# Queries, keys and values by one level of Strassen's recursion in a one-core streaming step

## The chip, the core and the metric

The kernel runs on one of the eight cores of a Trainium2 chip. The metric is the device time of one execution, in microseconds (us). A core has a matrix engine (TensorE, PE in the rows; PEld is its weight load), three engines for elementwise work (VectorE, DVE; ScalarE, ACT; GpSimd, POOL), and SyncE (SP), which here only issues DMAs. Matmul results land in PSUM; everything else lies in the on-chip SBUF or in DRAM.

## The reference

One layer of a hybrid encoder, for 2048 prompt tokens and 64 sample tokens (2112 in all), width 1024. The normalised input is multiplied by one wide weight, and the products feed two branches:

```python
xn = rms_norm(x, norm_gain)
u = xn @ w_in
xa, za, q, k, v, zb, ga, gb = split_in(u)          # 1024 columns each
...
q = rms_norm(q.reshape(B, T, H_B, 2, DK), q_norm_gain)   # groups of 64 columns
k = rms_norm(k.reshape(B, T, H_B, 2, DK), k_norm_gain)
v = v.reshape(B, T, H_B, DV)
...
m = jax.nn.sigmoid(ga) * (ya @ w_proj_a) + jax.nn.sigmoid(gb) * (yb @ w_proj_b)
y = x + m @ w_out
```

`ya` is a gated linear recurrence over `xa`, `yb` an eight-head differential attention over `q`, `k`, `v`. Everything is float32; k and v are outputs too.

## The kernel before

Each float32 operand is split into a rounded high part and a remainder, x = hi + lo, and each product is three matmuls (hi·hi, hi·lo, lo·hi): `mm3`, L68 to L71. The program has four stages: (A) L142 to L349, queries, keys and values; (B) L351 to L496, the five other column blocks and the recurrence; then the attention and the output projections. The change touches A and the first lines of B.

**Stage A.** 17 tiles of 128 tokens (the last has 64). Each is loaded (`norm_x`, L161), normalised, transposed by TensorE in eight pieces into PSUM (`turn_x`, L179) and split by ACT and DVE into `xh`, `xl`, which stay in SBUF through stage B. The weight comes in 12 blocks of 256 columns (`load_w`, L150): blocks 0 to 2 and 3 are values, 4 to 11 hold queries and keys of one head each. The order is 0, 1, 2, 4 to 11, 3 (L317). Per block and tile there are 8 slices of the contraction times 3 passes, 256 columns each: 12 × 17 × 24 = 4896 matmuls into the PSUM tile `acca`, which holds two token tiles. Values are copied out (L341, L342). Queries and keys are normalised per 64 columns (`norm_qk`, L200: square on ACT, sum on DVE, square root on ACT, reciprocal, a Newton step and a product on DVE), then transposed by TensorE (`turn_qk`, L226) and split into what the attention reads. The list `prev` holds one normalised accumulator back: the transposes of an accumulator are issued after the matmuls of the next one (L345).

**Stage B.** For each of eight groups n of 128 columns, five weights of 128 columns (`load_w1`, L357) meet the five token groups of `GROUPS` (512, 512, 384, 384, 320 wide) in `accb`: `hawk` for xa and za, and `gated` for zb, ga, gb (L489 to L494).

**Order.** TensorE's instructions run in the order in which the code emits them (`manual_schedule`, L113). The scheduler orders the other engines; SP takes the loads and stores in one queue, and an entry whose wait is not met holds back those behind it.

## Time and profile before

| | us |
|---|---|
| median of 3 runs | 3071.75 (3069.01 to 3071.79) |
| span of the profiled execution, first to last instruction | 3068.5 |
| stage A, first to last start of a matmul into `acca` | 14.0 to 662.3 |
| stage B, first to last start into `accb` | 663.2 to 1630.7 |
| TensorE busy | 2982.8 (97%) |
| DVE, ACT, POOL busy | 1322.6, 1135.1, 1065.5 |

The profiled execution's time is its span and some 3 us around it; the median of the runs stands 3.25 us above the span. A matmul's busy time overlaps its neighbours', so the distance between two starts, the pitch, is what one costs.

### The profile page before, as it was taken

How to read it: one execution, taken by the hardware profiler on the slowest of the kernel's cores; microseconds unless marked ns; L12 is line 12 of the kernel's file. 1: busy time of each engine (PE TensorE's matmuls, PEld its weight loads, DVE VectorE, ACT ScalarE, POOL GpSimd, SP SyncE). 2: the span in 40 equal slices, each digit the busy share in tenths (PEclk: the TensorE clock that was granted, in tenths of full speed). 3: DMA queues.
4: the chain of work that ended last, by engine and by line, in shares of the span. 5: the costliest groups of instructions: out<-in, count | busy, mean ns of one | idle time of the engine just before them, and what ended most of it. 6: DMA issues, size and time to landing. Idle time of an engine off the chain costs nothing.

```text
span 3068.5 us, 50185 instructions
## 1 busy us (share of the span) xinstructions
PE 2982.8 (97%) x19448; PEld 2787.9 (91%) x19448; DVE 1322.6 (43%) x3439; ACT 1135.1 (37%) x2179; POOL 1065.5 (35%) x1011
## 2 busy tenths in 40 slices
PE   7999999999999999999998999999999989999999
PEld 7999999999999998999896888888888889999999
DVE  7015454413314224133135667767776761232311
ACT  5112222213224223223134766676676651110100
POOL 1113233222212222122114666666666652222220
PEclk9999999999999999999999999999999999999999
DMA  5223333322121121121117344444543343433322
GB/s 173 81 83 115 125 124 129 120 83 72 39 75 58 43 83 50 45 77 42 64 47 212 107 143 128 127 138 135 147 115 123 94 155 110 122 118 90 94 94 91
DMA packets 208350, 312.37 MB, mean 102 GB/s; under 512 B 33760, under 2 KB 132944, under 8 KB 208112
## 3 DMA queue, kind: packets, MB, share of 16 engines
q1 hardware_dynamic: 203264, 299.10, 30.6%
q0 software_dynamic: 2608, 8.91, 1.0%
q8 instruction: 154, 2.52, 0.3%
q10 hardware_dynamic: 2240, 1.15, 0.1%
q14 instruction: 84, 0.69, 0.1%
HBM read 203.53 MB, written 105.41 MB: 101 GB/s over the span
## 4 chain that ended last, share of the span: by engine, by line
PE 84%; DVE 7%; ACT 3%; issue 2%; DMA 2%; POOL 1%; SPq 0%; POOLq 0%; ACTq 0%; DVEq 0%
PE accb L71 8%; PE accb L70 8%; PE accb L69 8%; PE acca L69 6%; PE acca L70 6%; PE acca L71 6%; PE acc L71 6%; PE acc L69 6%; PE acc L70 6%; PE accv L640 6%; PE pk L574 3%; PE pk L575 3%; PE ptt L632 3%; PE accv L763 2%; PE pk L695 1%
## 5 line engine op out<-in xcount | busy, mean ns | idle before, releaser
L71 PE MATMUL accb<-xh,wl 128*128 128x512 f32 (+2 forms) x1600 | 562.5, 352 | 0.0
L69 PE MATMUL accb<-xh,wh 128*128 128x512 f32 (+2 forms) x1600 | 562.3, 351 | 0.0
L70 PE MATMUL accb<-xl,wh 128*128 128x512 f32 (+2 forms) x1600 | 562.2, 351 | 0.0
L69 PE MATMUL acca<-wh,xh 128*128 128x256 f32 (+1 forms) x1632 | 469.1, 287 | 0.0
L70 PE MATMUL acca<-wl,xh 128*128 128x256 f32 (+1 forms) x1632 | 461.7, 283 | 2.1 <-DVE wl L131 1.6
L71 PE MATMUL acca<-wh,xl 128*128 128x256 f32 (+1 forms) x1632 | 461.3, 283 | 0.0
L71 PE MATMUL acc<-gh,wl 128*128 128x352 f32 x1152 | 373.6, 324 | 0.0
L69 PE MATMUL acc<-gh,wh 128*128 128x352 f32 x1152 | 373.1, 324 | 0.0
L70 PE MATMUL acc<-gl,wh 128*128 128x352 f32 x1152 | 370.8, 322 | 0.0
L69 PEld LDWEIGHTS accb<-xh,wh 128*128 128x128 f32 x1600 | 300.4, 188 | 25.6
L70 PEld LDWEIGHTS accb<-xl,wh 128*128 128x128 f32 x1600 | 300.3, 188 | 25.5
L71 PEld LDWEIGHTS accb<-xh,wl 128*128 128x128 f32 x1600 | 300.3, 188 | 25.3
L69 PEld LDWEIGHTS acca<-wh,xh 128*128 128x128 f32 (+1 forms) x1632 | 307.7, 189 | 5.4 <-ACT vst L341 3.8
L70 PEld LDWEIGHTS acca<-wl,xh 128*128 128x128 f32 (+1 forms) x1632 | 307.8, 189 | 2.8 <-DVE wl L131 1.8
L71 PEld LDWEIGHTS acca<-wh,xl 128*128 128x128 f32 (+1 forms) x1632 | 307.5, 188 | 0.0
L640 PE MATMUL accv<-v,tw 128*128 128x128 f32 x2176 | 295.3, 278 | 6.3 <-ACT o L652 6.2
L574 PE MATMUL pk<-k,Q 128*128 128x512 f32 (+2 forms) x640 | 266.3, 417 | 29.6 <-DVE mp L595 19.9
L56 POOL TENSOR_SCALAR wh<-raw 128x512 fp32r<-128x512 f32 x125 | 81.7, 654 | 607.9 <-PE accb L70 364.6
L587 DVE TENSOR_SCALAR_CACHE_REDUCE S<-pk,far 128x1024 f32<-128x1024 f32 x224 | 225.8, 1014 | 141.4 <-PE pk L575 131.5
L640 PEld LDWEIGHTS accv<-v,tw 128*128 128x128 f32 x2176 | 270.7, 194 | 10.9 <-ACT o L652 8.3
L605 ACT ACTIVATE S<-S,nm 128x1920 f32<-128x1920 f32 (+7 forms) x128 | 209.0, 1633 | 74.8 <-DVE nm L604 73.3
L575 PE MATMUL pk<-k,Q 128*128 128x512 f32 (+2 forms) x640 | 232.8, 369 | 1.0 <-DMA Q<-ql_d 1.0
(230 smaller groups left out, 5059.3 us busy)
## 6 DMA issues: line engine op xcount, KB each, us to landing
raw<-in_w1b SPq DMA_DIRECT2D x80, 256.0 KB, 2.9
raw<-in_ckT SPq DMA_DIRECT2D x32, 512.0 KB, 4.2
raw<-in_cv SPq DMA_DIRECT2D x32, 512.0 KB, 4.1
Q<-qh_d SPq DMA_DIRECT2D x126, 128.0 KB, 2.8
Q<-ql_d SPq DMA_DIRECT2D x126, 128.0 KB, 2.8
raw<-in_w1a SPq DMA_DIRECT2D x46, 256.0 KB, 3.0
gt<-ga_d SPq DMA_DIRECT2D x48, 176.0 KB, 2.6
rg<-yb_d SPq DMA_DIRECT2D x24, 352.0 KB, 3.1
```

What stands on the lines that cost most here:

```text
L56: nc.gpsimd.tensor_scalar(hi, src, 1.0, 1.0, op0=ALU.mult, op1=ALU.mult)
L69: nc.tensor.matmul(out, shi, mhi, start=start, stop=False)
L70: nc.tensor.matmul(out, shi, mlo, start=False, stop=False)
L71: nc.tensor.matmul(out, slo, mhi, start=False, stop=stop)
L574: nc.tensor.matmul(pk[:, o], Q[0][:, m, qs], kk, start=True, stop=False)
L575: nc.tensor.matmul(pk[:, o], Q[1][:, m, qs], kk, start=False, stop=True)
L587: nc.vector.tensor_scalar(s[:, k0 : k0 + f], pk[:, :f], far[:, h : h + 1], None, op0=ALU.add, op1=ALU.max, accum_out=mp[:, cx["j"] : cx["j ...
L605: nc.scalar.activation(s[:, :n], s[:, :n], AF.Exp, bias=nm, accum_out=sc[m])
L632: nc.tensor.transpose(ptt[:, j, :], ss[r][:, kt * P : (kt + 1) * P], ident)
L640: nc.tensor.matmul(acc[:, r, :], tw[:, j, :], hd[kt // 8][1][:, kt % 8, :], start=kt == r == 0, stop=kt == 2 * p + 1)
L695: nc.tensor.matmul(pk[:, us], Q, kc[:, us], start=True, stop=True)
L763: nc.tensor.matmul(acc, tw[:, j, :], vc[:, (j8 % 2) * 4 + j, :], start=j8 == 0 and j == 0, stop=False)
```

## The change

Values, and then queries with keys of heads 0 to 3 and of heads 4 to 7, become three groups g of 1024 columns. In each group the weight (1024 × 1024) and a pair of token tiles (t and t + 8) are cut into quarters: A11, A12 (tile t, first and second half of the contraction), A21, A22 (tile t + 8), B11 to B22. Seven products of sums and differences of quarters replace eight. A product is 4 slices × 3 passes = 12 matmuls of 512 columns. Eight pairs × 7 × 12 × 3 groups = 2016 matmuls; the sample's tile goes by the plain product, 60 matmuls in each group, 2196 in all. The order inside a group is `ITEMS` = 0, 1, 2, 3, "s", 4, 5, 6, 7.

The sums of quarters (S1 to S4 of x, T1 to T4 of the weight) are made on DVE and POOL and split again. `pair` issues the seven products; after each comes `fill`, which emits pieces of work that is due: steps of the next item's x (`x_steps`), at the end of a group steps of the next group's weight (`weight_steps`), and one entry of the list `later`, which holds the transposes of queries and keys. `done` is called as each of the four results C22, C11, C21, C12 comes up; for queries and keys one norm covers all four. In group 0 the normalised, transposed x is written to DRAM as `xn_d`; groups 1 and 2 read it back (`fetch_x`), and so does stage B (`take_x`), which now computes zb, ga and gb of n = 0 first, token group by token group. TensorE has 136 transposes of x, 272 of queries and keys and 8 small products (`strip_out`) in stage A, before and after.

```diff
+    xn_d = dram.tile([NT, P, KT, P], F32, name="xn_d")
...
+            wq = c.enter_context(tc.tile_pool(name="wq", bufs=17))
+            xo = c.enter_context(tc.tile_pool(name="xo", bufs=20))
+            sb = c.enter_context(tc.tile_pool(name="sb", bufs=13))
...
+            pm = c.enter_context(tc.tile_pool(name="pma", bufs=5, space=PSUM))
+            pt = c.enter_context(tc.tile_pool(name="pta", bufs=3, space=PSUM))
...
+            def cut(raw, fast, parts=2):
+                n = 4 // parts
+                hi = wq.tile([P, 4, 512], F32R, name="w8")
+                lo = wq.tile([P, 4, 512], F32R, name="w8")
+                for i in range(parts):
+                    s = slice(i * n, i * n + n)
+                    nc.scalar.copy(hi[:, s, :], raw[:, s, :])
+                    eng = nc.vector if fast or i % 2 == 0 else nc.gpsimd
+                    eng.tensor_tensor(lo[:, s, :], raw[:, s, :], hi.bitcast(F32)[:, s, :], op=ALU.subtract)
+                return hi, lo
...
+            def weight_steps(g, ws, fast):
+                src = I["wg"][g]
+                q = {}
+                parts = 4 if fast else 2
+                n = 4 // parts
+                def load(nm, i):
+                    q[nm] = quarter()
+                    for k in range(0, 4, 2):
+                        nc.sync.dma_start(q[nm][:, k : k + 2, :], src[i, :, k : k + 2, :])
...
+                return [
+                    lambda: load("B11", 0),
+                    lambda: load("B12", 1),
+                    lambda: sub("T1", "B12", "B11"),
+                    lambda: halve("B11", "B11"),
+                    lambda: load("B22", 3),
+                    lambda: load("B21", 2),
+                    lambda: sub("T2", "B22", "T1"),
+                    lambda: sub("T4", "B21", "T2"),
+                    lambda: halve("T2", "T2"),
+                    third,
+                    lambda: halve("T3", "T3"),
+                    lambda: halve("T1", "T1"),
+                    lambda: halve("B21", "B21"),
+                    lambda: halve("T4", "T4"),
+                    lambda: halve("B22", "B22"),
+                ]
...
+            def turn_x(t, half):
+                xt = xs[t][half]
+                ptx = pt.tile([P, 4, P], F32, name="ptx")
+                for j in range(4):
+                    nc.tensor.transpose(ptx[:, j, :tn], xt[:tn, j * P : (j + 1) * P], ident[:tn, :tn])
+                o = xo.tile([P, 4, P], F32, name="xq")
+                nc.vector.tensor_tensor(
+                    o[:, :, :tn], ptx[:, :, :tn],
+                    gain[:, half * 4 : half * 4 + 4].unsqueeze(2).to_broadcast([P, 4, tn]), op=ALU.mult,
+                nc.sync.dma_start(xn_d[t, :, half * 4 : half * 4 + 4, :tn], o[:, :, :tn])
+                return o
+            def fetch_x(t, half):
+                o = xo.tile([P, 4, P], F32, name="xq")
+                nc.sync.dma_start(o[:, :, :tn], xn_d[t, :, half * 4 : half * 4 + 4, :tn])
+                return o
...
+            def x_steps(item, first, xo_):
...
+                return [
+                    lambda: put("A11", lo, 0),
+                    lambda: put("A21", hi, 0),
+                    lambda: put("A22", hi, 1),
+                    lambda: (add(V, "S1", "A21", "A22", ALU.add), put("A12", lo, 1)),
+                    lambda: (add(V, "S2", "S1", "A11", ALU.subtract), s3()),
+                    lambda: (sp("A11", G), add(G, "S4", "A12", "S2", ALU.subtract)),
+                    lambda: (sp("S2", V), sp("S3", G)),
+                    lambda: (sp("S1", G), sp("A12", V), sp("A22", G), sp("S4", G)),
+                ]
+            def product(out, a, b, start, stop, m=P, more=False):
+                for kt in range(4):
+                    mm3(nc, out, a[0][:, kt, :m], a[1][:, kt, :m], b[0][:, kt, :], b[1][:, kt, :],
+                        start and kt == 0, stop and kt == 3, more)
...
+            def pair(x, w, done, fill):
+                b1 = pm.tile([P, 512], F32, name="acc")
+                product(b1, x["A11"], w["B11"], True, True)
+                p1 = small()
+                nc.scalar.copy(p1, b1)
+                fill()
+                b2 = pm.tile([P, 512], F32, name="acc")
+                product(b2, x["S2"], w["T2"], True, True)
+                u2 = small()
+                nc.vector.tensor_tensor(u2, p1, b2, op=ALU.add)
+                fill()
+                b3 = pm.tile([P, 512], F32, name="acc")
+                product(b3, x["S3"], w["T3"], True, True)
+                u3 = small()
+                nc.vector.tensor_tensor(u3, u2, b3, op=ALU.add)
+                fill()
+                b4 = pm.tile([P, 512], F32, name="acc")
+                product(b4, x["S1"], w["T1"], True, True)
+                c22 = small()
+                nc.vector.tensor_tensor(c22, u3, b4, op=ALU.add)
+                done(1, 1, c22)
+                fill()
+                product(b1, x["A12"], w["B21"], False, True, more=True)
+                c11 = small()
+                nc.scalar.copy(c11, b1)
+                done(0, 0, c11)
+                fill()
+                product(b3, x["A22"], w["T4"], False, True, more=True)
+                c21 = small()
+                nc.vector.tensor_tensor(c21, u2, b3, op=ALU.add)
+                done(1, 0, c21)
+                fill()
+                product(b4, x["S4"], w["B22"], False, True, more=True)
+                c12 = small()
+                nc.vector.tensor_tensor(c12, u2, b4, op=ALU.add)
+                done(0, 1, c12)
+                fill()
...
+            def out_qk(g, item):
+                h0 = 4 * (g - 1)
+                nb = 2 if item == "s" else 4
+                got = []
+                v = wk.tile([P, 32], F32, name="va")
+                def done(r, half, c):
+                    t = NT - 1 if item == "s" else item + 8 * r
+                    tn = TOK[t][1]
+                    sqv = small()
+                    nc.scalar.activation(sqv[:tn], c[:tn], AF.Square)
+                    i = len(got)
+                    nc.vector.tensor_reduce(
+                        v[:tn, 8 * i : 8 * i + 8], sqv[:tn].rearrange("p (g d) -> p g d", d=DK), axis=AX.X, op=ALU.add
+                    )
+                    got.append((half, t, c))
+                    if len(got) < nb:
+                        return
...
+                    for i, (isk, t, c) in enumerate(got):
+                        cv = c[:tn].rearrange("p (g d) -> p g d", d=DK)
+                        nc.vector.tensor_tensor(
+                            cv, cv, y[:tn, 8 * i : 8 * i + 8].unsqueeze(2).to_broadcast([tn, 8, DK]), op=ALU.mult
+                        )
+                        later.append(lambda isk=isk, t=t, c=c: turn_qk(h0, isk, t, c))
+                return done
...
+            norm_x(0)
+            norm_x(8)
+            wst = weight_steps(0, W[0], True)
+            for fn in wst[:2]:
+                fn()
+            X[0, 0] = {}
+            xst = x_steps(0, True, X[0, 0])
+            for fn in xst:
+                fn()
+            for fn in wst[2:]:
+                fn()
+            for g in range(NG):
+                for i, it in enumerate(ITEMS):
+                    nxt = (g, i + 1) if i + 1 < len(ITEMS) else (g + 1, 0)
+                    todo = []
+                    if nxt[0] < NG:
+                        X[nxt] = {}
+                        nit = ITEMS[nxt[1]]
+                        if nxt[0] == 0:
+                            for t in tiles_of(nit):
+                                norm_x(t)
+                        todo = x_steps(nit, nxt[0] == 0, X[nxt])
+                    if g + 1 < NG and i == 7:
+                        wnext = weight_steps(g + 1, W[g + 1], False)
+                        for fn in wnext[:3]:
+                            fn()
+                    more = wnext[3:] if g + 1 < NG and i == 8 else []
...
+                    def fill():
+                        for _ in range(2):
+                            if more:
+                                more.pop(0)()
+                        for _ in range(2 if nxt[0] > 0 else 1):
+                            if todo:
+                                todo.pop(0)()
+                        run_later()
+                    out = (out_v if g == 0 else out_qk)(g, it)
+                    (sample if it == "s" else pair)(X.pop((g, i)), W[g], out, fill)
+                    while more or todo:
+                        fill()
...
+            def take_x(g):
+                g0, gw = GROUPS[g]
+                for t in range(g0 // P, (g0 + gw + P - 1) // P):
+                    t0, tn = TOK[t]
+                    raw = hk.tile([P, 1092], F32, name=("R", "IX", "A")[t % 3])[:, : KT * P]
+                    raw = raw.rearrange("p (k t) -> p k t", k=KT)[:, :, :tn]
+                    nc.sync.dma_start(raw, xn_d[t, :, :, :tn])
+                    o = slice(t0 - g0, t0 - g0 + tn)
+                    nc.scalar.copy(xh[g][:, :, o], raw)
+                    nc.vector.tensor_tensor(xl[g][:, :, o], raw, xh[g].bitcast(F32)[:, :, o], op=ALU.subtract)
...
+            GATED = ((2, zb_d, True), (3, ga_d, False), (4, gb_d, False))
+            take_x(0)
+            w0 = [load_w1(j) for j, _, _ in GATED]
+            for g in range(1, len(GROUPS)):
+                take_x(g)
+            for g in range(len(GROUPS)):
+                for w, (j, dst, silu) in zip(w0, GATED):
+                    gate_out(mm_grp(w, g), dst, 0, silu, g)
+                hawk(n, load_w1(5 * n), load_w1(5 * n + 1))
...
+    wg = [quar(col(v, 0, 4), col(v, 4, 4))] + [quar(col(q, h, 4), col(k, h, 4)) for h in (0, 4)]
```

The end of a pair of queries and keys, on TensorE, before (an accumulator's end; `acca_2995` is two token tiles, `vst_2980` is the normalised accumulator before it):

```order
L70 MATMUL acca_2995<-wl_2820,xh1_99 128x256
L71 MATMUL acca_2995<-wh_2819,xl1_100 128x256
L232 MATMUL ptx_3059<-ident_70,vst_2980 128x128 [waits DVE_49,PE_49,Activation_49]
L232 MATMUL ptx_3059<-ident_70,vst_2980 128x128 x3
L69 MATMUL acca_3074<-wh_2801,xh1_99 128x256 [waits Activation_49]
L70 MATMUL acca_3074<-wl_2802,xh1_99 128x256
L71 MATMUL acca_3074<-wh_2801,xl1_100 128x256
```

And now: `acc_2491` takes the pair's last product, `s2_2504` is the same pair's C22, normalised, and `acc_2617` the next pair's first product.

```order
L70 MATMUL acc_2491<-w8_2144,xq_2308 128x512
L71 MATMUL acc_2491<-w8_2145,xq_2308 128x512
L72 MATMUL acc_2491<-w8_2144,xq_2309 128x512
L359 MATMUL ptx_2602<-ident_71,s2_2504 128x128 [waits DVE_49,PE_49]
L359 MATMUL ptx_2602<-ident_71,s2_2504 128x128 x3
L70 MATMUL acc_2617<-w8_1975,xq_2471 128x512
L71 MATMUL acc_2617<-w8_1976,xq_2471 128x512
L72 MATMUL acc_2617<-w8_1975,xq_2472 128x512 [waits Pool_49]
```

Before, the four transposes stood behind the matmuls of the next accumulator; now they stand right behind the last product of their own pair, and the next pair's products behind them.

The work of DVE at that place: from C12 (`s2_2584`), read from the last product, over the sums, the root and the Newton step to the normalised C22 (`s2_2504`).

```order
L322 TENSOR_TENSOR s2_2584<-s2_2434,acc_2491 128x512 [waits DMAHW3_49,PE_49]
L253 TENSOR_TENSOR xq_2694<-xq_2664,xq_2632 128x512 [waits DMAHW0_49,DVE_49]
L389 TENSOR_REDUCE va_2390<-s2_2586 128x8 [waits Activation_49]
L396 TENSOR_SCALAR va_2390<-va_2390 128x32 [waits DVE_49]
L401 RECIPROCAL ya_2592<-sra_2590 128x32 [waits Activation_49]
L62 SCALAR_TENSOR_TENSOR tmpa_2593<-ya_2592 128x32 [waits DVE_49]
L63 TENSOR_TENSOR tmpa_2593<-tmpa_2593,va_2390 128x32 [waits DVE_49]
L64 SCALAR_TENSOR_TENSOR ya_2592<-tmpa_2593,ya_2592 128x32 [waits DVE_49]
L405 TENSOR_TENSOR s2_2504<-s2_2504,ya_2592 128x512 [waits DVE_49]
```

C22's product with its norm now stands behind the last of the four results.

SP in the middle of the values, before: loads of x (`big`) two at a time ahead of the stores of values.

```order
L342 DMA out_v<-vst_453 128x512 [waits DMAHW1_49,Activation_49]
L164 DMA big_623<-in_x 128x1024 [waits DVE_49,PE_49]
L164 DMA big_681<-in_x 128x1024 [waits DMAHW3_49,DVE_49,PE_49]
L342 DMA out_v<-vst_565 128x512 [waits DMAHW4_49,Activation_49]
L164 DMA big_735<-in_x 128x1024 [waits DMAHW5_49,DVE_49,PE_49]
L164 DMA big_793<-in_x 128x1024 [waits DMAHW6_49,DVE_49,PE_49]
```

Now: `s2_500` and `s2_521` are C21 and C12 of one pair; `s2_548`, `s2_549` are the two halves of a tile of the second pair after it, and `s2_569`, `s2_570` those of its partner eight tiles on.

```order
L349 DMA out_v<-s2_500 128x2x256 [waits DMAHW4_49,DVE_49]
L197 DMA s2_548<-in_x 128x512 [waits DMAHW5_49]
L349 DMA out_v<-s2_521 128x2x256 [waits DMAHW6_49,DVE_49]
L197 DMA s2_549<-in_x 128x512 [waits DMAHW7_49,PE_49]
L197 DMA s2_569<-in_x 128x512 [waits DMAHW0_49,PE_49]
L197 DMA s2_570<-in_x 128x512 [waits DMAHW1_49,PE_49]
L223 DMA xn_d_67<-xq_610 128x512 [waits DMAHW2_49,DVE_49]
```

Three of the four halves stand behind the store of C12. On TensorE the transposes of `s2_548` follow the first product of the pair that comes next (`acc_590`); both halves go into the norm that they wait for.

SP at the passage to stage B: the last stores of keys and queries, the first weights of stage B (`raw`), and the reads of `xn_d` into `R`, `IX` and `A`.

```order
L375 DMA ql_d_58<-s2_6026 128x4x128 [waits DMAHW3_49,DVE_49]
L375 DMA out_kT<-s2_6036 128x4x128 [waits DMAHW4_49,Activation_49]
L375 DMA kh_d_59<-s2_6037 128x4x128 [waits DMAHW5_49,Pool_49]
L375 DMA kl_d_60<-s2_6038 128x4x128 [waits DMAHW6_49,Pool_49]
L532 DMA raw_6123<-in_w1b 128x512 [waits DMAHW7_49]
L532 DMA raw_6129<-in_w1b 128x512 [waits DMAHW0_49]
L673 DMA R_6083<-xn_d_67 128x1024 [waits DMAHW1_49]
L673 DMA IX_6087<-xn_d_67 128x1024 [waits DMAHW2_49]
L673 DMA A_6091<-xn_d_67 128x1024 [waits DMAHW3_49,PE_49]
L532 DMA raw_6612<-in_w1b 128x512 [waits DMAHW7_49,DMAHW4_49,Pool_49]
L532 DMA raw_6618<-in_w1b 128x512 [waits DMAHW5_49,DMAHW0_49,Pool_49]
L673 DMA R_6095<-xn_d_67 128x1024 [waits DMAHW6_49,DMAHW1_49,DVE_49]
```

Before, no x was read there; now the first three tiles stand behind the stores, and the fourth also behind the release of `R` by DVE.

## Rows read from the trace of the kernel before

**Rows 1.** The page, parts 1 and 4: busy time of each engine; the chain by engine.
```profile
PE 2982.8 (97%) x19448; PEld 2787.9 (91%) x19448; DVE 1322.6 (43%) x3439; ACT 1135.1 (37%) x2179; POOL 1065.5 (35%) x1011
...
PE 84%; DVE 7%; ACT 3%; issue 2%; DMA 2%; POOL 1%; SPq 0%; POOLq 0%; ACTq 0%; DVEq 0%
```

**Rows 2.** Tile acca: duration in ns min/median/max, first and last start, forms.
```profile
L69 PE MATMUL acca<-wh,xh x1632: 276/283/562, 14.0 to 662.1; 128*128 128x256 f32 x171, 128*64 128x256 f32 x11
```

**Rows 3.** The same view of tile accb.
```profile
L69 PE MATMUL accb<-xh,wh x1600: 305/334/499, 663.2 to 1630.4; 128*128 128x512 f32 x71, 128*128 128x384 f32 x71, 128*128 128x320 f32 x36
```

**Rows 4.** Timeline of PE at 300 us: start, duration, engine, line, instruction.
```profile
299.90 0.28 PE L69 MATMUL acca<-wh,xh 128*128 128x256 f32 x1
...
302.78 0.28 PE L69 MATMUL acca<-wh,xh 128*128 128x256 f32 x1
```

**Rows 5.** Timeline of PE at the start of the second stage.
```profile
664.01 0.40 PE L69 MATMUL accb<-xh,wh 128*128 128x512 f32 x1
...
667.42 0.39 PE L69 MATMUL accb<-xh,wh 128*128 128x512 f32 x1
```

**Rows 6.** Chain of waits, 0 to 60 us: start, duration, what.
```profile
2.60 7.96 DMA gain<-in_gain
...
32.89 1.07 PE ptx L186 x8
...
40.59 0.87 PE ptx L186 x8
```

**Rows 7.** Timeline of ACT at 533 us.
```profile
533.21 0.60 ACT L205 ACTIVATE sqa<-acca 128x512 f32<-128x512 f32 x1 [3.87 <-PE acca L71]
...
535.38 0.20 ACT L212 ACTIVATE sra<-va 128x8 f32<-128x8 f32 x1
```

**Rows 8.** Timeline of DVE at 533 us.
```profile
533.85 0.69 DVE L207 TENSOR_REDUCE va<-sqa 128x8 f32<-128x512 f32 x1 [2.51 <-ACT sqa L205]
...
536.05 0.17 DVE L63 TENSOR_TENSOR tmpa<-tmpa,va 128x8 f32<-128x8 f32 x1
...
536.25 0.59 DVE L64 SCALAR_TENSOR_TENSOR ya<-tmpa,ya 128x8 f32<-128x8 f32 x1
...
536.88 0.69 DVE L218 TENSOR_TENSOR vst<-acca,ya 128x512 f32<-128x512 f32 x1
```

**Rows 9.** Timeline of PE at 1788 us; in brackets idle time before, releaser.
```profile
1788.60 0.27 PE L802 MATMUL ptt<-ident,o 64*128 64x64 f32 x1
...
1793.44 1.12 PE L632 MATMUL ptt<-ident,S 128*128 128x128 f32 x4 [4.58 <-DVE yt L806]
```

**Rows 10.** Stretches around it: length, busy of PE, PEld, DVE, ACT, POOL, clock, DMA.
```profile
1781.00:1788.00 7.00, 6.63 (x52) 6.16 (x51) 5.04 (x27) 7.00 (x14) 5.67 (x18) 1.00 0.20 59
...
1793.00:1797.00 4.00, 3.56 (x17) 3.56 (x18) 1.85 (x6) 1.91 (x3) 1.58 (x2) 0.50 0.83 260
...
1797.00:1801.00 4.00, 4.00 (x29) 3.71 (x29) 1.90 (x6) 2.51 (x10) 0.00 (x0) 0.92 0.14 53
```

**Rows 11.** DMA, 0 to 663 us: rate in 40 slices; KB each, us to landing.
```profile
GB/s 249 169 177 187 36 109 48 48 124 78 62 80 100 93 103 131 161 80 153 105 135 153 81 134 131 129 82 129 183 81 112 157 125 96 138 145 94 97 48 48
...
raw<-in_w1a SPq DMA_DIRECT2D x46, 256.0 KB, 3.0
```

**Rows 12.** Groups of DVE, 0 to 663 us: busy us, mean ns.
```profile
L131 DVE TENSOR_TENSOR wl<-raw,wh 128x512 fp32r<-128x512 f32 x1 | 0.7, 671 | 0.0
```

**Rows 13.** Groups of POOL, 0 to 663 us.
```profile
L57 POOL TENSOR_TENSOR wl<-raw,wh 128x512 fp32r<-128x512 f32 x49 | 63.5, 1296 | 3.4
...
L56 POOL TENSOR_SCALAR wh<-raw 128x512 fp32r<-128x512 f32 x50 | 31.1, 622 | 236.5 <-PE acca L71 211.0 <-DMA raw<-in_w1a 25.1 <-DMA raw<-in_w1b 0.2
```

**Rows 14.** Timeline of SP's DMA queue at 540 us.
```profile
540.38 0.32 SPq L256 DMA_DIRECT2D qh_d<-big  x1
```

**Rows 15.** Timeline of DVE at 20 us.
```profile
20.02 1.16 DVE L63 TENSOR_TENSOR tmp<-tmp,v 128x1 f32<-128x1 f32 x1
```

**Rows 16.** Timeline of POOL at 20 us.
```profile
19.50 1.67 POOL L57 TENSOR_TENSOR wl<-raw,wh 128x512 fp32r<-128x512 f32 x1
```

More of the change, by code (lines that the diff above doesn't have):

```diff
@@ L64, in newton, with mm3 @@
         nc.vector.scalar_tensor_tensor(y, tmp, 1.5, y, op0=ALU.add, op1=ALU.mult)
[L68 to L71 removed]
+def mm3(nc, out, shi, slo, mhi, mlo, start, stop, more=False):
+    kw = dict(skip_group_check=True) if more else {}
+    nc.tensor.matmul(out, shi, mhi, start=start, stop=False, **kw)
+    nc.tensor.matmul(out, shi, mlo, start=False, stop=False, **kw)
+    nc.tensor.matmul(out, slo, mhi, start=False, stop=stop, **kw)
 @with_exitstack
@@ L159, in stream_step_kernel, with small @@
+            def small(dt=F32):
+                return sb.tile([P, 512], dt, name="s2")
             xs = {}
@@ new lines, in x_steps, with part, add, put @@
+            def x_steps(item, first, xo_):
+                q = {}
+                get = turn_x if first else fetch_x
+                V, G = nc.vector, nc.gpsimd
+                if item == "s":
+                    def part(i):
+                        a = get(NT - 1, i)
+                        xo_[f"A{i}"] = split_x(a, G, TS)
+                    return [lambda: part(0), lambda: part(1)]
+                lo, hi = item, item + 8
+                def add(eng, dst, x, y, op):
+                    if dst not in q:
+                        q[dst] = xo.tile([P, 4, P], F32, name="xq")
+                    eng.tensor_tensor(q[dst], q[x], q[y], op=op)
+                def put(nm, *a):
+                    q[nm] = get(*a)
+                def s3():
+                    q["S3"] = q["A21"]
+                    add(G, "S3", "A11", "A21", ALU.subtract)
+                def sp(nm, eng):
+                    xo_[nm] = split_x(q[nm], eng)
+                return [
[8 more added lines that the diff above has]
+                ]
@@ new lines, in sample @@
+            def sample(x, w, done, fill):
+                b1 = pm.tile([P, 512], F32, name="acc")
+                product(b1[:TS], x["A0"], w["B11"], True, False, TS)
+                fill()
+                product(b1[:TS], x["A1"], w["B21"], False, True, TS)
+                c1 = small()
+                nc.scalar.copy(c1[:TS], b1[:TS])
+                done(0, 0, c1)
+                fill()
+                b2 = pm.tile([P, 512], F32, name="acc")
+                product(b2[:TS], x["A0"], w["B11"], True, False, TS)
+                product(b2[:TS], x["A0"], w["T1"], False, False, TS)
+                fill()
+                product(b2[:TS], x["A1"], w["B22"], False, True, TS)
+                c2 = small()
+                nc.scalar.copy(c2[:TS], b2[:TS])
+                done(0, 1, c2)
+                fill()
@@ L348, in stream_step_kernel @@
-            while prev:
-                turn_qk(*prev.pop(0))
+            NG = 3
+            ITEMS = [0, 1, 2, 3, "s", 4, 5, 6, 7]
+            tiles_of = lambda it: [NT - 1] if it == "s" else [it, it + 8]
+            warm = gp.tile([1, 1], F32, name="warm")
+            nc.vector.memset(warm, 1.0)
+            nc.scalar.activation(warm, warm, AF.Sqrt)
+            W = [{} for _ in range(NG)]
+            X = {}
+            norm_x(0)
+            norm_x(8)
+            wst = weight_steps(0, W[0], True)
@@ new lines, in stream_step_kernel @@
+            while later:
+                run_later()
+        xnp = c1.enter_context(tc.tile_pool(name="xnp", reuse_waits=RW, bufs=1))
+        xh, xl = [], []
+        for g, (g0, gw) in enumerate(GROUPS):
+            xh.append(xnp.tile([P, KT, gw], F32R, name=f"xh{g}"))
+            xl.append(xnp.tile([P, KT, gw], F32R, name=f"xl{g}"))
+        wp = c1.enter_context(tc.tile_pool(name="wp", reuse_waits=RW, bufs=7))
+        wr = c1.enter_context(tc.tile_pool(name="wr", reuse_waits=RW, bufs=2))
```

286 lines of the change are left out of this document (107 added, 179 removed).

## The prediction, before the changed kernel was run

> **What bounds the kernel now.** I read the page first, then the tile view of the two accumulators of stages A and B, then timelines inside them. TensorE is busy 97% of the span and carries 84% of the chain that ended last [rows 1]: whatever stage A saves or loses on TensorE reaches the end. Stage A's matmuls run from 14.0 to 662.3 us, stage B's begin at 663.2 [rows 2, 3]. Inside A the matmuls follow each other without a gap: 24 of them, 299.90 to 302.78, take 2.88 us, a pitch of 0.120 us for 256 columns [rows 4]. Of the 663 us, 4896 × 0.120 = 587.5 are matmuls; 408 transposes, eight in 0.87 us [rows 6], are 44.4; the strips about 1; some 30 are left, nearly all at the start (TensorE runs on end only from about 33 us [rows 6]). So A has no slack but its start, and every microsecond that TensorE waits in the new A is a loss.
>
> What hides the norms of queries and keys in A today is the list that holds one accumulator back: the norm's chain has the next accumulator's 48 matmuls (5.8 us) to run beside. That is the thing to look for in the new order.
>
> **The change part by part.**
>
> *Matmuls.* 2196 instead of 4896, but of 512 columns. Stage B has that form: 15 steps from 664.01 to 667.42, 3.41 us, a pitch of 0.227 [rows 5]. 2196 × 0.227 = 498.5, so 498.5 − 587.5 = **−89**. The transposes and strips are as many as before: 0. Seven eighths of the products would give a little more; the sample by the plain form costs the difference.
>
> *The end of a pair of queries and keys.* By the order the four transposes of C22 stand right behind the pair's last product, and C22's product with its norm stands behind the sums of all four results, the last of which comes from that last product. TensorE can do nothing else meanwhile: the next pair's products stand behind the transposes. The chain: C12 added on DVE (0.69, as the product out of PSUM at 536.88), then square, sum, root, reciprocal, Newton step, product. In the trace the same chain goes from 533.21 to 536.88 + 0.69 = 537.57, 4.36 us with its handovers [rows 7, 8]; with the addition 5.0. Of the pair's other results all but the last step is done by then. So TensorE idles about 5.0 us.
>
> An idle time of that length has a second price. At 1788 us TensorE waited 4.58 us [rows 9]; before it the granted clock was 1.00, in 1793 to 1797 it was 0.50 (1.2 GHz instead of 2.4) and in 1797 to 1801 0.92 [rows 10]. At half speed for about 4.2 us, 2.1 us of work are lost. A stall then costs 7.1 us. In two groups of eight pairs, 16 × 7.1 = 114. The sample's two ends have a shorter chain (64 tokens, two results), which I put at 6.5 each, 13. Together **+127**. Bounds: 16 × 4.4 + 8 = 78 without the clock and with the rows' bare chain; 16 × 9 + 16 = 160 if POOL's work delays it as below.
>
> *Values.* In group 0, x is still to be loaded and normalised. By SP's order three of the four halves of a later pair stand behind the store of the C12 of an earlier one, and TensorE wants the tile's transposes right after the first product of the next pair. From the end of that C12's product: addition 0.7, store's and load's issue 0.32 each [rows 14], landing 3.0 for 256 KB [rows 11], square 0.6, sum, root, reciprocal and Newton step about 1.5, scaling 0.6, handovers 0.5: about 7.5 us. TensorE has one product of 12 × 0.227 = 2.7 us to do in that time and idles 4.8, then runs at half speed as above: 6.9. Seven items of the group are loaded so: **+48**. Bounds: 7 × 2 = 14 (the stores' wait met early) and 7 × 9 = 63.
>
> *The start.* Before the second product, DVE has 16 differences of weights, 28 remainders, 4 scalings by the gain and 4 pieces of x: 52 × 0.68 = 35.4 us at the 0.671 of the remainder in the trace [rows 12]. It starts when 2.25 MB have landed: at 249 GB/s [rows 11] 9.0 us after the first loads at 2.6 [rows 6], 11.6. POOL makes seven pieces of 1.3 us [rows 13] from SBUF beside it, which I count with 6 us more, and gaps with 4. By DVE's order the norm of tiles 1 and 9 stands behind all remainders, and TensorE wants tile 1's transposes after its first product. So it begins in earnest at about 59 us and has done 3 us of its work by then: 56 lost against some 30 now, **+26** (bounds +10, if x's norm comes earlier, and +36).
>
> *Change of weights.* Twice, between groups, the next weight is cut while the last pair runs: POOL 7 × 2.6 + 6 × 1.3 (twice the 512-column piece [rows 13]) = 26 us, DVE about 19, beside 34 us of TensorE's work. It should fit, but the pool of weight tiles has 17 places and 14 are in use, so the pieces come in step with the products: 5 us each, **+10** (0 to +20).
>
> *Passage to stage B.* Before, x was there and the gap at 663 us was nothing. Now the first tile's read stands on SP behind the last stores of keys, whose POOL pieces are 4 × (0.62 + 1.30) = 7.7 us [rows 13]; then a load of 512 KB (about 3.5, between the 3.0 of 256 KB [rows 11] and twice that), the split on ACT and DVE (1.2 and 1.4), and a fourth tile that reuses the buffer of the first, another load and split. Around 23 us on the chain, of which TensorE covers little: **+22** (10 to 28). What remains of stage B is the same matmuls in another order: 0, TensorE has them all on end today.
>
> Sum: −89 + 127 + 48 + 26 + 10 + 22 = +144, span 3068.5 + 144 = 3212.5. The median of the runs stands 3.25 above the profiled span, so **3216 us**. All lows give +23 (−89 + 78 + 14 + 10 + 0 + 10), 3095; all highs +218 (−89 + 160 + 63 + 36 + 20 + 28), 3290. It is not likely that all err to one side.
>
> **The rivals.**
>
> *POOL in the way of the norm (slower still).* At 19.50 POOL's remainder took 1.67 us; a Newton step's product of one column beside it took 1.16 us [rows 15, 16], while one of eight columns took 0.17 at 536.05, and the next step 0.59 at 536.25 [rows 8]. In the new stage A POOL works on pieces of the next x at just those ends of pairs. If two or three of the chain's steps wait 0.8 us each, 25 stalls grow by 2: +50, 3266. Against it: in most of the chain's place POOL may have run out of pieces. The Trainium skill has the rule ("SBUF — State Buffer", section "Who interferes with whom"): a DVE instruction with two inputs in SBUF contends with a GpSimd instruction that reads SBUF, and who starts first holds the other for its whole length. The row at 20.02 agrees with it.
>
> *The clock isn't lost.* Only the idle time counts: 25 × 2.1 = 52 less, 3163. For it: the rows at 1788 are from another kind of work, with small transposes and gaps on either side. Against it: the stall is as long.
>
> *The waits are hidden: faster.* If the norm of a pair didn't hold TensorE, because the transposes come late enough or the chain is done while a product still runs, only the low bounds of start and passage are left: −89 + 10 + 10 = −69, 3003. The point from which it decides: with start, weights and passage at 58, 25 stalls must stay below (89 − 58) / 25 = 1.2 us each. For it: TensorE's other work is dense. Against: the order shows no matmul between the last product and the transposes that wait for it, and the rows' chain alone is 4.36.
>
> *The change does only part of what it says.* If 512-column matmuls cost more here than in B, as the weight side changes with nearly each one, −89 shrinks; but B's also change it with each [rows 5], so this is only a part of the range.
>
> **How the numbers follow.** My forecast, 3216 with stalls at about 7 us, has 57%, and its own range is 3180 to 3250. Clock not lost, about 3163: 17%. POOL in the way, about 3266: 17%. A slower one of small stalls, 3080 to 3140: 4%. Faster, about 3003: 4%. No difference: 1%. A range of 3140 to 3275 leaves out the last three and the ends of the second and third. About 0.2% is what a measurement of this kernel can tell from no change (its runs lie within 3 us). Faster by more than that: 0.04; within: 0.01; slower: 0.95.
>
> **What would show it.** In the new profile TensorE's idle time before the transposes of C22 (L359), released by DVE's product L405, 16 times about 5 us; before the transposes of x in group 0 (L217) about 4.8, released by ACT's scaling; granted clock well below 0.9 in all of stage A and near 0.5 behind each stall. Matmuls of A at a pitch of 0.227. The first long run of products at about 59 us; the last product of A at about 662 + 122 = 784, and the first start into `accb` about 22 us behind it. I am wrong if L217 and L359 wait under 2 us, if the clock stays at 1.00 behind them, or if stage A's matmuls have another pitch.

## The result: 7.3% slower, and where the time went

The changed kernel takes 3294.79 us (median of four runs, 3289.33 to 3301.9) against 3070.45 before: a ratio of 1.073 (95% interval 1.072 to 1.075). Forecast were 3216, within 3140 to 3275: the direction was right, the loss 79 us too small, and the time lies outside the range. The profiled execution took 3301.9, the longest of the four; its span is 3300.0.

The page after, parts 1 and 4, against [rows 1]:

```profile
PE 2973.9 (90%) x16748; PEld 2649.8 (80%) x16748; DVE 1520.8 (46%) x3428; ACT 1291.8 (39%) x2341; POOL 1249.0 (38%) x1030
...
PE 66%; DVE 6%; DMA 2%; ACT 2%; POOL 1%; issue 1%; SPq 0%; DVEq 0%; ACTq 0%; POOLq 0%
```

TensorE is busy for almost the same time, but in a longer span, and it carries 66% of the last chain instead of 84%. What it waits for, in us in total, times, longest (the view of waits, TensorE alone):

```profile
PE ptx L359 <- DVE s L405: 125.8, 19, 27.2
PE ptx L217 <- ACT s L209: 71.8, 10, 18.6
...
PE accb L70 <- ACT xh L675: 20.9, 1, 20.9
...
PE acc L72 <- POOL xq L236: 9.8, 2, 8.8
PE acc L70 <- DVE s L307: 8.4, 1, 8.4
PE pk L780 <- DMA Q<-ql_d: 7.4, 1, 7.4
PE acc L70 <- DVE s L302: 7.0, 1, 7.0
PE pk L779 <- DMA k<-kl_d: 6.5, 1, 6.5
```

The first two are the forecast's waits: transposes of queries and keys for the product with their norm, transposes of x for its scaling. By stretches (columns as in [rows 10]): start, values, first change of weights, queries and keys, passage to stage B, start of the attention. After, and then the stretches of before that answer to the first, to all of A, and to the last:

```profile
0.00:59.00 59.00, 12.65 (x38) 9.60 (x39) 42.05 (x83) 32.08 (x67) 15.94 (x13) 1.00 0.50 165
59.00:270.00 211.00, 174.99 (x746) 137.38 (x746) 81.03 (x170) 71.83 (x156) 68.58 (x51) 0.89 0.30 102
270.00:342.00 72.00, 45.27 (x178) 35.95 (x177) 65.03 (x83) 29.17 (x42) 44.86 (x24) 0.84 0.37 122
342.00:853.00 511.00, 393.89 (x1663) 306.46 (x1661) 265.51 (x388) 180.87 (x306) 219.70 (x179) 0.87 0.39 117
853.00:874.00 21.00, 0.24 (x2) 0.00 (x0) 4.86 (x5) 4.88 (x6) 12.37 (x12) 0.50 0.92 309
...
1843.00:1900.00 57.00, 34.37 (x132) 24.57 (x131) 32.70 (x84) 22.05 (x32) 28.21 (x29) 0.73 0.77 203
```

```profile
0.00:33.00 33.00, 14.23 (x81) 12.49 (x82) 21.14 (x48) 16.31 (x34) 11.27 (x17) 0.95 0.62 210
33.00:663.00 630.00, 630.00 (x5239) 622.52 (x5240) 254.95 (x703) 156.34 (x388) 161.41 (x231) 1.00 0.31 110
...
1631.00:1690.00 59.00, 45.41 (x228) 33.86 (x227) 42.28 (x126) 32.48 (x56) 29.64 (x21) 0.88 0.77 214
```

Before, TensorE had no idle microsecond from 33 to 663, at a granted clock of 1.00. Length less PE busy gives the idle time of each stretch. For the clock I laid the matmuls beside the records of the granted clock: between 59 and 853 us TensorE worked 124 us at half speed, so 62 were lost. With that the 231.5 us between the two spans come out so, within 1 us (waits as in the view; 5.6 us taken as the usual wait at an end; all half clock behind 270 us stands with the ends; stage B is taken from the first to the last start into `accb`, 874.1 and 1843.0, before 663.2 and 1630.7):

| term | forecast | measured |
|---|---|---|
| matmuls and transposes, without what the clock costs | −89 | −79 |
| start: idle 46.3 against 18.8 | +26 | +27.5 |
| values: idle 36.0, clock 17.2 | +48 | +53 |
| ends of queries and keys: idle 101, clock 45 | +127 | +146 |
| two changes of weights: idle 26.7 + 27.2 less two usual waits | +10 | +43 |
| passage to stage B | +22 | +21 |
| stage B | 0 | +1.4 |
| behind stage B (1457.0 against 1437.8) | 0 | +19.2 |

One end of a pair, TensorE and then DVE after, as in [rows 8] and [rows 9]:

```profile
512.74 1.09 PE L359 MATMUL ptx<-ident,s 128*128 128x128 f32 x4 [6.38 <-DVE s L405]
```

```profile
507.69 0.68 DVE L322 TENSOR_TENSOR s<-s,acc 128x512 f32<-128x512 f32 x1
508.29 1.44 DVE L253 TENSOR_TENSOR xq<-xq 128x512 f32<-128x512 f32 x1
509.65 0.67 DVE L389 TENSOR_REDUCE va<-s 128x8 f32<-128x512 f32 x1
...
511.45 0.19 DVE L63 TENSOR_TENSOR tmpa<-tmpa,va 128x32 f32<-128x32 f32 x1
511.68 0.19 DVE L64 SCALAR_TENSOR_TENSOR ya<-tmpa,ya 128x32 f32<-128x32 f32 x1
511.90 2.50 DVE L405 TENSOR_TENSOR s<-s,ya 128x512 f32<-128x512 f32 x4
```

The chain from C12's sum to C22's product is there, 507.69 to about 512.5. The Newton steps take 0.19: POOL isn't in their way here. Two sums of x pieces (L253) lengthen the wait to 6.4: one stands ahead of C12's sum, and DVE waited 1.3 us there for the piece's load; one (1.44 beside POOL, 0.69 without) stands in the middle. Where no such sum is in the chain the wait is 4.5. Over the pairs the waits run from 4.5 to 6.4, and to 8.6 and 27.2 at the changes of weights.

### The profile page after: what moved, and what is told of

The parts are those of the page before. It is cut to its first block, busy times and chain, and to the rows that moved or that the text cites. A ratio compares the mean times of both kernels' runs of the same rounds, so it can differ in the third digit from the quotient of the medians.

```text
span 3300.0 us, 45408 instructions
## 1 busy us (share of the span) xinstructions
PE 2973.9 (90%) x16748; PEld 2649.8 (80%) x16748; DVE 1520.8 (46%) x3428; ACT 1291.8 (39%) x2341; POOL 1249.0 (38%) x1030
## 4 chain that ended last, share of the span: by engine, by line
PE 66%; DVE 6%; DMA 2%; ACT 2%; POOL 1%; issue 1%; SPq 0%; DVEq 0%; ACTq 0%; POOLq 0%
PE accb L71 9%; PE accb L70 9%; PE accb L72 9%; PE acc L70 6%; PE acc L72 6%; PE acc L71 6%; PE accv L845 5%; PE pk L779 3%; PE pk L780 3%; PE ptt L837 2%; PE accv L968 2%; DVE S L792 1%; DVE cf L816 1%; PE pk L900 1%; PE ptt L955 1%
## 5 line engine op out<-in xcount | busy, mean ns | idle before, releaser
L70 PE MATMUL accb<-xh,wh 128*128 128x384 f32 (+2 forms) x1600 | 563.3, 352 | 20.9 <-ACT xh L675 20.9
L71 PE MATMUL accb<-xl,wh 128*128 128x384 f32 (+2 forms) x1600 | 563.4, 352 | 0.4 <-DVE xl L676 0.4
L72 PE MATMUL accb<-xh,wl 128*128 128x384 f32 (+2 forms) x1600 | 563.3, 352 | 0.0
L70 PE MATMUL acc<-w,xq 128*128 128x512 f32 (+1 forms) x732 | 319.3, 436 | 18.8 <-DVE s L307 8.4
L72 PE MATMUL acc<-w,xq 128*128 128x512 f32 (+1 forms) x732 | 303.9, 415 | 9.8 <-POOL xq L236 9.8
L71 PE MATMUL acc<-w,xq 128*128 128x512 f32 (+1 forms) x732 | 306.1, 418 | 0.0
L818 POOL TENSOR_TENSOR S<-S,S 128x2048 f32<-128x2048 f32 (+3 forms) x64 | 230.6, 3604 | 4.6
L236 POOL TENSOR_TENSOR xq<-xq 128x512 fp32r<-128x512 f32 (+1 forms) x126 | 173.8, 1388 | 126.1 <-ACT xq L235 43.8
L71 PEld LDWEIGHTS acc<-gl,wh 128*128 128x128 f32 x1152 | 219.6, 191 | 0.0
L70 PEld LDWEIGHTS acc<-gh,wh 128*128 128x128 f32 x1152 | 216.8, 188 | 0.0
```

The source lines that it names most:

```text
L70: nc.tensor.matmul(out, shi, mhi, start=start, stop=False, **kw)
L71: nc.tensor.matmul(out, shi, mlo, start=False, stop=False, **kw)
L72: nc.tensor.matmul(out, slo, mhi, start=False, stop=stop, **kw)
L236: eng.tensor_tensor(lo[:, :, :w], a[:, :, :w], hi.bitcast(F32)[:, :, :w], op=ALU.subtract)
L818: nc.gpsimd.tensor_tensor(S[0][:, :n], S[0][:, :n], S[1][:, :n], op=ALU.add)
```

## The experiments

Each run is set against 3294.8, the changed kernel's median, whose own runs differ by 12 us; where a few us matter, the traces decide. They can: what lies behind stage B takes 1441 to 1457 us in versions whose edits don't touch it, but stage B's first matmul, at 874.1 in the changed kernel, comes at 873.9 and 871.2 in the two runs whose edits leave stage A's products alone.

**The clock by itself.** `w` is the weight in use, 20 matmuls fill the wait:

```diff
                 done(0, 1, c12)
+                if w is not W[0]:
+                    spin(x["S4"][0][:, 0, :], w["B22"][0][:, 0, :])
                 fill()
```

> The transposes stay where they are, but 20 matmuls of 512 columns on data at hand, whose result nobody reads, stand ahead of them at each of the 16 pairs' ends (4.5 us at full speed). Theory (clock): a stall costs its idle time and about 2.2 us of half clock behind it; the chain takes as long as before, TensorE isn't idle in it, the granted clock stays at 1.00, and about 16 x 2.2 = 35 us go: 3260. Rival (only the idle time counts): no change, 3295, within 6 us. If the useless matmuls make the stall longer, slower by up to 16 us.

3259.7, 35 us less by doing more. Its waits at the same transposes (L366 here), and the stretch of queries and keys:

```profile
PE ptx L366 <- DVE s L412: 46.1, 15, 22.7
```

```profile
342.00:850.00 508.00, 443.13 (x1999) 348.73 (x1998) 273.25 (x399) 192.46 (x318) 236.77 (x192) 0.94 0.45 136
```

The mean granted clock rises from 0.87 to 0.94, and work that nobody needs shortens the run. By the records of the clock, half speed cost 35 us in the pairs away from the changes of weights in the changed kernel, and costs 4 here. That a stall costs its idle time and then some 2.2 us of clock is shown; that only idle time counts is refuted.

**The place of the transposes.** A flag lets the last fill of an item and the first of the next pass over `later`:

```diff
-                fill()
+                fill(False)
```

> Theory (the norm's chain): the transposes of queries and keys wait for a chain of about 5.6 us behind their own pair's last product; with two products of the next pair (5.4 us) ahead of them the wait is covered. In the changed kernel's trace these waits are 98 us of idle time over both groups, and some 40 us more go to the halved clock behind them; about 120 us should go, 3295 to some 3175, and the waits at L359 under 1 us each outside the change of weights. Rival (buffers): the results are held longer in a pool of 13 tiles, so DVE and ACT wait for free tiles and TensorE for PSUM: the idle time moves to the products, and less than 50 us go.

3215.2, 80 us less: between the two. Waits at L359 fall from 125.8 to 65.6, 22.5 of them at the second change of weights; at ten ends 3 to 8 us stay. At 480 us DVE and POOL show why:

```profile
480.19 0.90 DVE L62 SCALAR_TENSOR_TENSOR tmpa<-ya 128x32 f32<-128x32 f32 x1
481.13 1.19 DVE L63 TENSOR_TENSOR tmpa<-tmpa,va 128x32 f32<-128x32 f32 x1
```

```profile
479.25 1.80 POOL L253 TENSOR_TENSOR xq<-xq 128x512 f32<-128x512 f32 x1 [6.48 <-DVE xq L253]
481.00 1.27 POOL L236 TENSOR_TENSOR xq<-xq 128x512 fp32r<-128x512 f32 x1
```

With TensorE at work again, the pieces of the next x come into the chain, and steps of 0.19 take 0.90 and 1.19 beside POOL. Of the 54 Newton steps of stage A, 26 take over 0.3 us here; in the changed kernel three do, two of them at the changes of weights. The rival of the forecast (POOL in the way) is real, but in this version, hardly in the changed kernel. The waits at the products are as long as in the changed kernel, so buffers didn't hold it.

**A norm for each result**, transposes three products later:

```diff
-                    if len(got) < nb:
-                        return
...
+                    later.append((fills[0], lambda: turn_qk(h0, half, t, c)))
```

> Each of the four results gets a norm of its own as soon as it is there (four short chains instead of one for all four), and its transposes come three products later. Theory (the wait for the last of four results makes the stall): the waits at L359 go outside the changes of weights, more of them than in the run with the transposes put off alone, where 3 to 5 us were left at 9 of 16 ends since the one chain stood between DVE's pieces of x: 3165 to 3185. Rival (DVE is what is short in this stage): 12 more short DVE instructions per pair, some 3 us, make the products wait for their sums: 3215 or more.

3210.4: neither number; nearer to the rival's. By the traces it is better than its median: stage B begins 89 us earlier than in the changed kernel, where putting the transposes off gave 79; what lies behind stage B took 10 us longer in this run. 44.5 us of waits at the transposes (L361 here) are left in 16 pieces, the longest, 15.9, at a change of weights, all of them for DVE. So the wait for the fourth result was the stall; taking it away another way leaves DVE's queue as the next limit.

**Loads of x.** The norm of the item after the next is emitted when the next item's x is transposed:

```diff
+                        if len(todo) <= low:
+                            while ahead:
+                                norm_x(ahead.pop(0))
```

> The loads of x in the values' group are emitted as soon as the x tiles of the next item are transposed, one half pair earlier, ahead of the stores of C21 and C12. Theory (order on SP's queue): the waits at L217 of about 5 us, 34 us in all, and the 17 us of half clock behind them go: 45 us, 3250. Rival (the loads wait for free tiles, or the norm's chain is too long anyway): the waits stay at 3 us or more each, less than 15 us.

3254.8, 40 less, 36 of them ahead of stage B by the traces. Of the seven waits of 3.9 to 5.4 us behind the start one (5.5 us) stays, and four become 1.3. The order on SP's queue made them; in the changed kernel the loads for the transposes at 113 us follow the store of C12:

```profile
105.88 0.37 SPq L349 DMA_DIRECT2D out_v<-s  x1
106.30 1.81 SPq L197 DMA_DIRECT2D s<-in_x  x3
```

**Changes of weights: remainders on DVE alone.**

```diff
-                    eng = nc.vector if fast or i % 2 == 0 else nc.gpsimd
+                    eng = nc.vector
```

> At the change of weights all remainders are made on DVE instead of half of them on POOL. Theory (DVE and POOL hold each other up when both read two operands from SBUF: in the changed kernel's trace a piece of 1024 columns takes 1.21 on DVE and 2.33 on POOL alone, and up to 3.4 on DVE beside POOL): the two sum up, and 7 x 2.33 = 16 us of POOL per change become 7 x 1.21 = 8.5 us of DVE; the 27 us wait at the second change falls to about 19, and both changes together give 12 to 18 us: 3280. Rival (DVE is the full one): its queue gets longer by 8.5 us per change, the wait rises to 35, slower by about 15: 3310.

3288.4, 6 less; by the traces the stretch around the first change is 6 us shorter and that around the second 4, 10 together. The second change's wait falls from 27.2 to 22.7, the first's idle time by 4. Remainders (L139) of the second change, 555 to 595 us and here 545 to 587 (one piece on each engine lies ahead of that), count, busy, mean ns: changed kernel's DVE, its POOL, this version's DVE:

```profile
L139 DVE TENSOR_TENSOR w<-w,w 128x1024 fp32r<-128x1024 f32 x6 | 13.5, 2257 | 0.0
```

```profile
L139 POOL TENSOR_TENSOR w<-w,w 128x1024 fp32r<-128x1024 f32 x6 | 17.3, 2896 | 4.0 <-ACT w L137 4.0
```

```profile
L139 DVE TENSOR_TENSOR w<-w,w 128x1024 fp32r<-128x1024 f32 x12 | 15.7, 1348 | 0.0
```

Twelve pieces on DVE alone take 15.7 us; six of them beside POOL's six took 13.5. Two engines were no faster than one: they hold each other up. But it is less than the 12 to 18 us expected, and a quarter of what the changes cost (next run): most of the wait has another cause.

**Changes of weights left out.**

```diff
-                        wnext = weight_steps(g + 1, W[g + 1], False)
-                        for fn in wnext[:3]:
-                            fn()
-                    more = wnext[3:] if g + 1 < NG and i == 8 else []
+                        W[g + 1] = W[g]
+                    more = []
```

> Both changes of weights are left out: groups 1 and 2 multiply by the values' weight, so queries and keys are other numbers; the products, norms, transposes and stores stay. Theory (the changes are what the forecast mis-sized, at 5 us each): the waits of 18 us at the products near 287 to 317 us go, the waits at L359 near 332 and 567 fall from 8.6 and 27.2 to the usual 5 to 6, and with the half clock behind them 42 to 50 us go: 3248. Rival (the changes are mostly covered, and the waits there come from the first reads of x and the constants): less than 20 us go.

3253.4, 41 less, and the longest wait at L359 is 8.4:

```profile
PE ptx L359 <- DVE s L405: 104.5, 18, 8.4
```

The two changes cost 41 to 43 us, not 10. What fills the time stands in the traces. From the end of one wait at L359 to the end of the next, the pair at the second change, first in the changed kernel, then without the change:

```profile
542.90:594.40 51.50, 24.29 (x102) 19.10 (x103) 44.41 (x38) 23.69 (x33) 38.72 (x18) 0.73 0.39 116
```

```profile
516.20:546.70 30.50, 24.11 (x102) 18.94 (x102) 15.40 (x25) 11.00 (x19) 12.78 (x11) 0.89 0.42 127
```

TensorE's share is the same 24 us. DVE has 15 us of its own work with the pair and the next x, and the weights add 29: 44.4, without a pause of more than 1 us from 556 us on. The last sum of the norm comes behind a remainder in that queue, and the transposes wait for it:

```profile
586.26 3.35 DVE L139 TENSOR_TENSOR w<-w,w 128x1024 fp32r<-128x1024 f32 x1
589.54 0.67 DVE L389 TENSOR_REDUCE va<-s 128x8 f32<-128x512 f32 x1
```

With all remainders on DVE it is still busy for 41.5 us of 47.1.

**The start of the attention.** Six more small tiles in the ring `wp` ahead of stage B's first weight (six times `wh` and `wl`, eight columns set to zero).

> Six small tiles more are written in the ring of seven from which stage B's weights come, so that its last weight lies where it lay in the kernel before. In the changed kernel the second load of queries (low parts) for the attention's first pair wants the memory of a remainder that the last matmul of stage B reads, and is issued at 1843.6 instead of 16 us before that stage's end. Theory (the ring's phase): the load is issued beside the first ones at about 1829, TensorE's waits of 7.4 and 6.5 us at the start of the attention go, and with the half clock behind them 15 to 20 us: 3277. Rival (the attention starts late for its keys, which come behind more stores): the waits stay, within 5 us of 3295.

POOL issues these loads; the first row is the changed kernel's, the second this one's:

```profile
1843.60 0.60 POOL L753 DMA_DIRECT2D Q<-ql_d  x1 [14.28 <-PE accb L72]
```

```profile
1829.10 0.62 POOL L756 DMA_DIRECT2D Q<-ql_d  x1
```

In the median 7 us less (3287.4); from stage B's last matmul to the end 1443.3 instead of 1457.0. In the first 20 us of that TensorE is idle for 6.0 us instead of 13.9; before it was 6.6, and in every version without these tiles it is 13.9 to 14.5. Stage A no longer draws its weights from this ring, so stage B's last remainder came to lie where the first queries go. The remaining 5 us against before weren't traced further; they are within the 16 us by which this stretch differs between runs.

**The start, and the passage.** The norms of tiles 1 and 9 ahead of the remainders; stage B's first x through ACT's queue:

```diff
+            norm_x(1)
+            norm_x(9)
             for fn in wst[2:]:
```

```diff
-                    nc.sync.dma_start(raw, xn_d[t, :, :, :tn])
+                    (nc.scalar if g == 0 else nc.sync).dma_start(raw, xn_d[t, :, :, :tn])
```

> The norms of tiles 1 and 9 are emitted ahead of the other weights' differences and remainders. Theory (DVE's order): TensorE's wait of 18.6 to 23 us at L217 at the start goes; TensorE then waits for each product's weight remainders instead, whose sum stays; 8 to 14 us are left of the gain: 3284. Rival (DVE's whole sum sets the start): the same total, the wait moves to the products, 0 to 4 us.

> The reads of x for the first token group of stage B go through ACT's queue instead of SP's, where they stand behind ten stores and two loads. Theory (SP's queue holds them): the first read is issued at about 854 instead of 860.5, the wait of 21 us at the entry shrinks by 6 to 8: 3288. Rival (the memory that they are read into comes free late, or the split after it is what takes the time): less than 2 us.

3290.7 and 3294.4. At the start 46 us of idle time up to 60 us become 33, and a wait of 9.5 follows at 68. By the traces 14 us are gained in the first two products and 8 lost behind them, so 6 stay: between the two expectations, most of it as the rival says, by DVE's sum. At the passage the wait is 19.7 instead of 20.9, as the rival says. The edit isn't a clean test of SP's order, though: the first read is issued at 855.6 instead of 860.5, but on ACT's queue the fourth, which reuses the first one's buffer, stands behind the split of the third tile and is issued at 866.5 instead of 868.8. What stays on that path is two reads and two splits, one after the other.

**Together.** Three versions, each with the ring, the loads, the remainders on DVE and the early norms.

> Together: x loaded earlier, transposes of queries and keys three products later (two of the next pair's fills passed over, strips in their place), remainders at the change of weights on DVE alone, norms of tiles 1 and 9 first, x for stage B through ACT's queue, the ring's phase as before. If the named waits are all there is and add up, 40 + 130 + 7 + 18 + 10 + 7 = 212 us go from 3295: 3083, within 15 us of the kernel before (3070). If the waits only move on to the next resource (tiles held longer, DVE full), at most half goes: 3190 or more.

> The version of all edits again, with a norm for each result, the next pair's x read in one step and its sums a product later (in the last version DVE stood up to 3.8 us at a sum whose x hadn't landed, in the middle of the norm's chain), and four buffers instead of three for stage B's first x. The last version leaves 97 us of idle time from 60 us to the start of stage B, and 22 of half clock. If the sums' wait is what held the chain, 25 idle and 10 of the clock go, and 5 at the entry: 3100. If the changes of weights and the entry are all that is left, 3130. To beat the kernel before (3071) 70 must go.

> The edits of the first combined version with one norm for the four results, the next pair's x read in one step and its sums a product later, and stage B's x through SP's queue with three buffers, as in the changed kernel. If DVE's stand at sums whose x hadn't landed is what lengthened the norm's chain (3.1, 3.7, 5.3, 3.9, 4.1 us at five ends in the first combined version), 20 us of idle time and 8 of half clock go: 3141 becomes 3115. If the norm for each result was what cost in the second combined version, but the reads don't matter: 3140.

3141.5 (ratio to before 1.023, 1.021 to 1.025), 3166.4 (1.030, 1.029 to 1.032) and 3127.2 (1.018, 1.016 to 1.019). The first gave back 153 of the hoped 212 us. The second fell short: with four buffers the wait at the passage is 28.3 instead of 18.9 (on ACT the split of the fourth tile, whose read was issued at 740.1, stands at 752.8 behind that of the next group's first tile, which waited for its read), and with the norm for each result there are 20 small waits at the transposes. In the third, sums that no longer stand in the chain bring 14 us, half of what was expected. Its largest waits (L370 are the transposes of queries and keys):

```profile
PE ptx L370 <- DVE s L416: 39.2, 9, 12.1
PE ptx L217 <- ACT s L209: 32.1, 7, 14.5
PE accb L70 <- ACT xh L694: 24.0, 1, 24.0
```

No version beats the kernel before. In the third, idle time and half clock in stage A still come to some 132 us more than before: 17 at the start, 26 with the values, 35 at the ends of queries and keys, 23 at the changes of weights and 30 at the last end and the passage. That outweighs 79 us of matmuls saved.

## Why the prediction was right in kind and too low

- *Matmuls*: right in mechanism; −79 without the clock, forecast −89. Some 5 of the 10 are the first 24 matmuls: they lie 0.427 us apart, at half speed, where the trace has no record of the clock (they begin at 59 us). The pitch elsewhere is the forecast's, three steps in 0.68 us (timeline of TensorE after):

```profile
300.10 0.39 PE L70 MATMUL acc<-w,xq 128*128 128x512 f32 x1
...
300.78 0.39 PE L70 MATMUL acc<-w,xq 128*128 128x512 f32 x1
```

- *The end of a pair*: right. The wait is 5.6 in the mean where 5.0 was said, for sums of x in the chain, and the half clock behind it 2.3 where 2.1 was (35 us over the 15 ends away from the changes): 146 for 127 with the half clock at the changes. That the clock isn't lost is refuted by the run that fills the wait.
- *Values*, *start* and *passage*: right within 5 us, with the places named. The start's terms add up to 57 and not to the 59 that is said, so its 26 hit in part by luck. At the passage the loads and splits one after the other are there; that SP's queue costs something of its own wasn't confirmed.
- *Change of weights*: this is the step that failed, 43 us for 10. "It should fit" set POOL's 26 and DVE's 19 us beside 34 of TensorE's. Three things are wrong with it. The pair beside which the weight is cut has 84 × 0.227 = 19 us of products, 24 with transposes and half clock, not 34. DVE's own 15 us with each pair weren't counted. And the 19 became 29, since the two engines hold each other up: a remainder of 1024 columns takes 2.26 on DVE and 2.90 on POOL there, against 1.35 on DVE when POOL has none. I had the row for the last one [rows 15, 16] and used it only for the rival at the pairs' ends. It is the smaller part: with the remainders taken off POOL 10 of the 42 us went. That DVE's full queue makes the rest is read from the traces; no run lightened that queue by itself.
- *The rest of stage B*, "the same matmuls in another order: 0", and nothing behind it: right by itself (1.4), but 19 us were lost behind it, 14 of them in the first 57 us, where the six tiles more took 12 away. The forecast didn't ask where stage B's last tiles lie in memory and who waits for them next.
- The range: the two failed terms had 0 to 20 and no bound at all. The profiled span was missed by 87.5 us (3300.0 for 3212.5); these two are 52 of them, the ends 19, the matmuls 10.

The Trainium skill's rule that was weighed there ("SBUF — State Buffer", section "Who interferes with whom": a DVE instruction with two inputs in SBUF contends with a GpSimd instruction that reads SBUF) agrees with the rows at the change of weights (2.26 in the mean for 1.35) and in the run with the transposes put off (1.19 for 0.19).

## What to carry to other kernels

Before fewer matmuls are bought with more sums on other engines, ask for each place where TensorE's order has no other work behind a wait: one such wait of 5 us cost 8 here, and 18 of them more than the products saved. Before work is said to fit beside a stage, add to it what its engine already does there, and add up DVE's and POOL's work on SBUF operands as one queue, not as two. And when a stage draws fewer tiles from a ring, look at whose memory the next stage's first loads want.

## What was not expected of the hardware

Twenty matmuls without a use at each of 16 stalls made the kernel 35 us faster, for the clock they kept up. And 12 remainders on one engine (15.7 us) were nearly as fast as six each on two (13.5 and 17.3).
